# Eight value buffers in a dilated-attention branch, weight splits moved behind a copy, and a reordered last pair of Strassen products

## The chip, the cores and the metric

The kernel runs on one core of one Trainium2 chip. The time is the device time of one execution in microseconds (us); before the change it is 2152.53 us, the median of 3 runs (2151.78 to 2155.79).

## The reference, cut to what matters

A decoder trunk of two residual layers works on 1024 tokens of width 1024, all in float32. Each layer is a token mixer and then a gated MLP. The first layer's mixer puts a chunked gMLP and a mixture of dilated attentions side by side; the second layer's mixer is a gated linear attention.

```
h = rms_norm(x, norm_mix_g[layer])
mix = even_mixer(...) if layer % 2 == 0 else gla_mixer(...)
x = x + mix
h = rms_norm(x, norm_ffn_g[layer])
x = x + (silu(causal_dwconv(h @ w_gate, conv_w, conv_b)) * (h @ w_up)) @ w_down
```

Two places of it matter here. In `even_mixer` eight heads of width 64 take q, k and v from one projection; q and k are normalised, and every query attends to a near window (128 keys back) and to dilated windows. In the MLP the gate and up projections have 2816 columns each.

## The kernel before, in words

**Numbers.** Every matrix product is made of float32r parts: an operand is split into a rounded part and the rest (`split`, lines 101 and 102: a copy on ScalarE, a subtraction on VectorE; `scaled`, lines 106 and 107, also multiplies by a gain), and three of the four products of parts are summed (`PASSES`), so that one 128-row step costs three matmuls.

**Order of the instructions.** The program is traced in the order of the code, and the framework then sets each engine's own order when the program is built, by a simulated timeline: what is traced first goes first, but what is ready sooner in the simulation may overtake. Two calls fix parts of that order. `tc.keep_in_program_order(ins)` puts an instruction behind the one traced before it on its engine. `tc.issue_after(ins)` puts all instructions of a block that run on the engine of `ins` behind `ins`; it is an order, not a wait for a result, and it binds that engine alone. Tiles come from pools; a tile with `bufs=k` has k slots, and a new tile waits until the last reader of the old one in its slot is done.

**The attention (`attention`, called by `even`).** The eight heads are taken as four pairs. `project(p)` does one pair. For each of eight blocks of 128 tokens, `projected(n)` multiplies with the pair's weights into a PSUM bank `pj` (line 193 through `mm_tok`; two banks of that tag, two more for the first pair), squares q and k on ScalarE (line 780), copies the values scaled into `vN` (line 782; six slots), stores them to DRAM (line 785), and normalises q and k in place on VectorE (line 789, which reads the same `pj` bank). The loop over `n` then makes a near-branch "unit": q and k are split, transposed (lines 809 and 817), scored (line 727), masked (line 732), exponentiated (line 733), transposed again (line 747) and multiplied with the value tiles `vN[n-1]` and `vN[n]` into a bank `po` (line 755). Every fourth unit is followed by a copy of `po` (line 828). The first pair is traced three blocks ahead (`lead`). Then `dilated(p)` does the other branch, with values read back from DRAM, while the projection of the next pair is traced after it.

The weights of pair p come from `load_qkv`: four loads into `raw` buffers (line 111; four slots in all), each split into two tiles. Pairs 0 and 2 put their first four tiles in a pool of their own, `wx` (four slots), all others go to the shared eight-slot pool `w`. So the splits for the third pair can begin as soon as the first pair has finished with its `wx` tiles.

**The MLP's gate and up products (`ffn_up`).** Two blocks of 128 columns of one matrix, against 1024 tokens, are one two-by-two step of Winograd's form of Strassen's method: seven products, numbered 1 to 7 (`step(p)`, line 293), on three banks. Product 2 has bank A; 5 and then 3 add up in bank C; 1, 6, 7 and 4 add up in bank B, and between each two of these ScalarE copies the partial sum out of the bank (lines 297, 301, 305 and 308), which the next product must wait for. Product 3 is read from bank C by VectorE (line 310). The units alternate gate and up (`todo`, 22 of them per layer). In the middle ones product 1 of the next unit is traced between 7 and 4. The first unit (gate, whose followers' first products were made earlier) and the last (up) have nothing there:

```
            if 0 < i < len(todo) - 1:
                nxt = stream(*todo[i + 1])
                nxt[0](1)
            step(4)
            step(3)
```

After a gate unit comes the convolution (`conv`, lines 320 to 323); after an up unit the product of both (line 378), the right sides of the down projection and their stores. `ffn_down` (line 400) follows in new PSUM pools over the same banks.

Of the kernel before, what the change touches and what calls it, by code (L numbers as in the profile page):

```python
# [9 lines left out]
F32 = mybir.dt.float32  # L10
# [9 lines left out]
P = 128  # L20
# [20 lines left out]
PASSES = ((0, 0), (0, 1), (1, 0))  # L41


def f32(ap):
    return ap.bitcast(F32)
# [11 lines left out]
def trunk(ctx: ExitStack, tc: tile.TileContext, a, out):  # L57
    nc = tc.nc
    V, A, G, T, Q = nc.vector, nc.scalar, nc.gpsimd, nc.tensor, nc.sync
# [49 lines left out]
    def load_raw(src, name, cols=D):  # L109
        raw = rawp.tile([P, D], F32, tag="raw", name=name)[:, :cols]  # L110
        Q.dma_start(raw, src)
        return raw
# [128 lines left out]
    def ffn_up(l, T3, ps, pool, norm_end):  # L241
        cw = pool.tile([P, NF, 3], F32, name=f"cw{l}")
        Q.dma_start(cw, a["conv_w"][l])
        cb = pool.tile([P, NF], F32, name=f"cb{l}")
        Q.dma_start(cb, a["conv_b"][l])
        right = {1: hq[0][0], 2: hq[1][0], 3: hq[1][1], 4: hq[0][1], 5: T3[0], 6: T3[1], 7: T3[2]}

        def stream(kind, f):

            raws = [load_raw(w_of(kind)[l, f + i], f"r{kind}{f + i}") for i in range(2 if f else 1)]  # L250
            A11, A12, A21, A22 = (raws[i][:, c] if f or not i else None for i in range(2) for _, c in HALVES)
            out = pool.tile([P, 2, S], F32, tag=kind, bufs=1, name=f"{kind}{f}")
            (C11, C12), (C21, C22) = ([out[:, i, c] for _, c in HALVES] for i in range(2))
            s1 = pool.tile([P, 512], F32, tag="s1", bufs=2, name=f"s1{kind}{f}")
            sums, bank, made = {}, {}, {}

            def summed(name, x, y, op):
                sums[name] = pool.tile([P, 512], F32, tag="S", bufs=4, name=f"{name}{kind}{f}")
                G.tensor_tensor(sums[name], x, y, op=op)  # L259
                return sums[name]  # L260

            def left(p):
                if p == 5:
                    return summed("S1", A21, A22, ALU.add)
                if p == 6:
                    return summed("S2", sums["S1"], A11, ALU.subtract)
                if p == 7:
                    return summed("S3", A11, A21, ALU.subtract)
                if p == 3:
                    return summed("S4", A12, sums["S2"], ALU.subtract)  # L270
                return {1: A11, 2: A12, 4: A22}[p]

            def prep(p):
                if f == 0 and p > 2:
                    w = wp.tile([P, 2, 512], F32R, tag="w", name=f"w{kind}{f}p{p}")
                    Q.dma_start(f32(w), sided[l][kind, p])
                    made[p] = [w[:, i, :] for i in range(2)]
                else:
                    made[p] = parts_of(left(p), f"w{kind}{f}p{p}")

            def step(p):
                if p not in made:
                    prep(p)
                L = made[p]

                b = {2: "A", 5: "C", 3: "C"}.get(p, "B")
                more = b in bank
                if not more:
                    bank[b] = ps.tile([P, 512], F32, tag="pt" if b == "A" else "m1", name=f"p{kind}{b}{f}")
                o = bank[b]  # L290
                for j in range(4):
                    for ii, jj in PASSES:
                        T.matmul(o, L[ii][:, j * P : j * P + P], right[p][:, jj, j, :], skip_group_check=more,  # L293
                                 start=(not more and j == 0 and (ii, jj) == PASSES[0]),
                                 stop=(j == 3 and (ii, jj) == PASSES[-1]))
                if p == 1:
                    A.copy(s1, o)
                elif p == 2:
                    V.tensor_add(C11, s1, o)
                elif p == 6:  # L300
                    A.copy(C12, o)
                elif p == 5:
                    A.copy(C22, o)
                elif p == 7:
                    A.copy(s1, o)  # L305
                    V.tensor_add(C22, C22, s1)  # L306
                elif p == 4:
                    A.copy(C21, o)  # L308
                elif p == 3:
                    V.tensor_add(C12, C12, o)  # L310

            return step, out, prep

        def conv(f, g2):
            ts = []
            for i in range(2):
                g = g2[:, i, :]
                t = pool.tile([P, S], F32, tag="t", bufs=4, name=f"t{f + i}")
                w = lambda j: cw[:, f + i, j : j + 1]
                A.activation(t, g, AF.Identity, bias=cb[:, f + i : f + i + 1], scale=w(2))  # L320
                V.scalar_tensor_tensor(t[:, 1:], g[:, : S - 1], w(1), t[:, 1:], op0=ALU.mult, op1=ALU.add)  # L321
                V.scalar_tensor_tensor(t[:, 2:], g[:, : S - 2], w(0), t[:, 2:], op0=ALU.mult, op1=ALU.add)  # L322
                A.activation(t, t, AF.Silu)  # L323
                ts.append(t)
            return ts

        def put(dst, f, p, src):
            Q.dma_start(dst[l][p][f // 4][:, f // 2 % 2, :], src)

        def down_weights(f):  # L330

            ra, rb = (load_raw(a["w_down"][l, f + i], f"rd{f + i}") for i in range(2))
            A11, A21, A12, A22 = ra[:, :512], ra[:, 512:], rb[:, :512], rb[:, 512:]
            S = {p: pool.tile([P, 512], F32, tag="S", bufs=4, name=f"D{p}{f}") for p in (5, 6, 7, 3)}
            V.tensor_add(S[5], A21, A22)
            V.tensor_sub(S[6], S[5], A11)
            V.tensor_sub(S[7], A11, A21)
            V.tensor_sub(S[3], A12, S[6])
            for p in S:
                put(wsd, f, p, S[p])  # L340

        def down_acts(f, t0, t1):

            (B11, B12), (B21, B22) = ([t[:, c] for _, c in HALVES] for t in (t0, t1))
            x, y = (pool.tile([P, 2, 512], F32, tag="t", bufs=4, name=f"{n}{f}") for n in "xy")
            right = {1: B11, 2: B21, 3: B22, 5: x[:, 0], 6: x[:, 1], 7: y[:, 0], 4: y[:, 1]}
            V.tensor_sub(right[5], B12, B11)
            V.tensor_sub(right[6], B22, right[5])
            V.tensor_sub(right[7], B22, B12)
            V.tensor_sub(right[4], B21, right[6])  # L350
            for p in right:
                put(actd, f, p, right[p])

        todo = [(kind, f) for f in range(0, NF, 2) for kind in "gu"]
        cur, nxt = stream(*todo[0]), stream(*todo[1])
        for step, _, _ in (cur, nxt):
            step(1)
            step(2)
            if step is cur[0]:
                for prep, p in ((nxt[2], 1), (nxt[2], 2), (cur[2], 5)):  # L360
                    prep(p)
                norm_end()
        for i, (kind, f) in enumerate(todo):
            step, out, _ = cur
            early = (1, 2) if i < 2 else (1,)
            for p in (5, 6, 2, 7):
                if p not in early:
                    step(p)
            if 0 < i < len(todo) - 1:
                nxt = stream(*todo[i + 1])  # L370
                nxt[0](1)
            step(4)
            step(3)
            if kind == "g":
                ts = conv(f, out)
            else:
                for j in range(2):
                    V.tensor_mul(ts[j], ts[j], out[:, j, :])
                down_acts(f, *ts)
                down_weights(f)  # L380
            cur = nxt
# [333 lines left out]
    def attention(ps, at, av, pq, pq0, par0, wx, wq0, gqk, masks, rest, gm_open):  # L715
# [46 lines left out]
        def project(p, ws=None, then=None, early=None):  # L762


            ws = ws or load_qkv(p, wx)
            pool = pq if p % 2 else pq0
            qR = pool.tile([P, 2, S], F32R, tag="qR", bufs=1, name=f"qR{p}")
# [2 lines left out]
            vN, os, qns = [], [], []  # L770
            heads = lambda t: t.rearrange("p (h c) -> p h c", c=64)

            def projected(n):
# [4 lines left out]
                qn = pq.tile([P, 256], F32, tag="qn", bufs=5, name=f"qn{p}{n}")  # L778
                rn = r0[:, n : n + 1]
                A.activation(qn, pj[:, :256], AF.Square, scale=rn)  # L780
                vN.append(pq.tile([P, P], F32, tag="vN", bufs=6, name=f"vN{p}{n}"))
                got = A.mul(vN[n], pj[:, 256:384], rn)
                if early:
                    early(n, got)
# [12 lines left out]
            for n in range(NT):  # L797
# [22 lines left out]
                if n % 4 == 0:  # L820
                    ot, po = outputs(f"{p}n{n}")
# [3 lines left out]
                     lambda s, i: kT[:, 2 * s + i, :].rearrange("p (r m) -> p r m", r=4)[:, :, 32 * m0 : 32 * n + 32],  # L825
                     vN[m0 : n + 1], mband, lambda t: t.rearrange("p (m r) -> p r m", r=4))
                if n % 4 == 3:
                    A.copy(ot[:, :, :P], po)
                if then and n in (4, 5):
                    then(n - 4)  # L830
            v4 = av.tile([P, 4, 2, P], F32, tag="v4", name=f"v4{p}", bufs=1)
# [33 lines left out]
        def combined(p, g, os, den, e):  # L865
# [11 lines left out]
            V.tensor_add(o0, o0, o1)  # L877
            Q.dma_start(bcat[g].rearrange("(n p) c -> p n c", p=P)[:, :, p * P : p * P + P], o0)

        made = project(0, wq0, early=rest)  # L880
        for p in range(PAIRS):
            os, *qkv = made
# [482 lines left out]
```

## Time and profile before

| | before |
|---|---|
| median of 3 runs | 2152.53 us |
| the profiled execution | 2153.15 us |
| its span from first to last instruction | 2151.4 us |
| mean granted TensorE clock over the span | 0.999 |
| TensorE matmul busy | 2126.6 us (99%) |
| VectorE busy | 1526.0 us (71%) |
| ScalarE busy | 1035.9 us (48%) |
| GpSimd busy | 482.4 us (22%) |

The profile is of one execution. PE is TensorE (PEld its weight loads), DVE VectorE, ACT ScalarE, POOL GpSimd, SP the engine that issues the DMAs. A group or timeline row gives the start and the duration in us, the engine, the line, the operation, the tile written and the tiles read, and in brackets how long the engine had been idle before it and what ended that. Matmuls overlap in the array, and their ends are modelled. A row of the view by windows gives the length of a stretch, the busy time of each engine in it with the number of instructions, and then the granted TensorE clock as a share of full speed, the share of DMA time and the GB/s.

### The profile page before, as it was taken

The numbers are of one execution on the slowest core, as the hardware profiler recorded it, in microseconds if no ns is written. First come the engines' busy times: TensorE is split into PE (matmuls) and PEld (weight loads), VectorE is DVE, ScalarE is ACT, GpSimd is POOL, SyncE is SP. The second block draws the span as 40 slices with busy tenths as digits, with TensorE's granted clock in tenths as the row PEclk, the third lists the DMA queues.
The fourth block names the chain that finished last, engine by engine and source line by source line (L and its number), as shares of the span: only waits on it lengthen the run. The fifth ranks groups of instructions, "written<-read, shape, count | busy, mean of one in ns | idle before, by whom it ended". The sixth has DMA issues, their size and how long they took to land.

```text
span 2151.4 us, 29696 instructions
## 1 busy us (share of the span) xinstructions
PE 2126.6 (99%) x10444; PEld 1804.0 (84%) x10444; DVE 1526.0 (71%) x2451; ACT 1035.9 (48%) x1998; POOL 482.4 (22%) x521
## 2 busy tenths in 40 slices
PE   8999999999999999999999999999999999999999
PEld 7999988888888888888898888888788888888887
DVE  7566655587888888655577777677778888885554
ACT  7555664365444444444454455535544444444443
POOL 5344310012424334000010011011234334220000
PEclk9999999999999999999999999999999999999999
DMA  7022313754444544765553233395554544457664
GB/s 273 24 77 68 104 40 120 256 195 156 155 161 158 176 143 157 255 237 192 206 183 113 74 105 102 133 307 206 177 167 161 168 153 154 162 181 280 215 216 166
DMA packets 159413, 353.70 MB, mean 164 GB/s; under 512 B 17392, under 2 KB 54256, under 8 KB 158880
## 3 DMA queue, kind: packets, MB, share of 16 engines
q1 hardware_dynamic: 159264, 351.81, 47.9%
q8 instruction: 82, 1.34, 0.3%
q14 instruction: 67, 0.55, 0.1%
HBM read 243.15 MB, written 108.59 MB: 163 GB/s over the span
## 4 chain that ended last, share of the span: by engine, by line
PE 92%; DVE 2%; ACT 2%; DMA 2%; issue 1%; SPq 0%; POOL 0%; DVEq 0%; ACTq 0%
PE puB L293 11%; PE pgB L293 11%; PE po L193 8%; PE pv L193 6%; PE pj L193 6%; PE puC L293 6%; PE pgC L293 6%; PE pdB L400 5%; PE pdC L400 5%; PE pdO L400 4%; PE puA L293 3%; PE pgA L293 3%; PE pdQ L400 2%; PE pdP L400 2%; PE pu L193 2%; PE pBq L1070 2%
## 5 line engine op out<-in xcount | busy, mean ns | idle before, releaser
L102 DVE TENSOR_TENSOR da<-ar,da 128x512 fp32r<-128x512 f32 x154 | 106.1, 689 | 154.2 <-ACT da L101 154.1
L101 ACT CAST da<-ar 128x512 fp32r<-128x512 f32 x154 | 95.9, 623 | 207.8 <-PE pdC L400 91.5
L193 PE MATMUL po<-wo,hq 128*128 128x512 f32 x768 | 184.0, 394 | 0.2 <-ACT hq L101 0.2
L193 PEld LDWEIGHTS po<-wo,hq 128*128 128x128 f32 x768 | 141.6, 188 | 29.6 <-DVE hq L102 1.1
L193 PE MATMUL pv<-wv,hq 128*128 128x512 f32 (+2 forms) x768 | 140.8, 340 | 1.6 <-DVE b L1102 1.6
L400 PE MATMUL pdB<-dw,da 128*128 128x512 f32 x528 | 135.5, 391 | 0.9 <-ACT u L308 0.7
L400 PE MATMUL pdC<-dw,da 128*128 128x512 f32 x528 | 135.1, 390 | 0.0
L193 PEld LDWEIGHTS pv<-wv,hq 128*128 128x128 f32 x768 | 118.7, 189 | 16.4 <-DVE b L1102 2.1
L400 PEld LDWEIGHTS pdB<-dw,da 128*128 128x128 f32 x528 | 98.7, 188 | 22.3 <-ACT u L308 1.1
L259 POOL TENSOR_TENSOR S1g<-rg 128x512 f32<-128x512 f32 x20 | 31.1, 1555 | 382.9 <-DMA wsd<-D 266.1
L400 PEld LDWEIGHTS pdC<-dw,da 128*128 128x128 f32 x528 | 99.0, 188 | 20.5
L102 DVE TENSOR_TENSOR dw<-wr,dw 128x512 fp32r<-128x512 f32 x154 | 105.6, 686 | 12.1 <-ACT dw L101 11.9
L193 PE MATMUL pj<-wq,hq 128*128 128x384 f32 x576 | 111.3, 341 | 0.0
L141 POOL TENSOR_SCALAR rn<-ssq 128x1 f32<-128x1 f32 x24 | 9.7, 403 | 446.1 <-ACT h L149 244.9
L101 ACT CAST dw<-wr 128x512 fp32r<-128x512 f32 x154 | 95.0, 617 | 15.7 <-DMA wr<-in_w_dn 9.3
L400 PE MATMUL pdO<-dw,da 128*128 128x512 f32 x396 | 102.2, 389 | 0.2 <-DVE dw L102 0.2
L193 PEld LDWEIGHTS pj<-wq,hq 128*128 128x128 f32 x576 | 99.9, 189 | 0.1
L400 PEld LDWEIGHTS pdO<-dw,da 128*128 128x128 f32 x396 | 74.2, 188 | 16.0 <-DVE dw L102 0.6
L322 DVE SCALAR_TENSOR_TENSOR t<-g,cw,t 128x1022 f32<-128x1022 f32 x44 | 76.6, 1742 | 0.1
L306 DVE TENSOR_TENSOR g<-g,s1g 128x512 f32<-128x512 f32 x22 | 16.2, 737 | 76.9 <-ACT s1g L305 76.9
L321 DVE SCALAR_TENSOR_TENSOR t<-g,cw,t 128x1023 f32<-128x1023 f32 x44 | 58.2, 1322 | 16.2 <-ACT t L320 16.1
L323 ACT ACTIVATE t<-t 128x1024 f32<-128x1024 f32 x44 | 46.7, 1061 | 29.7 <-DVE t L322 29.6
(1084 smaller groups left out, 5432.6 us busy)
## 6 DMA issues: line engine op xcount, KB each, us to landing
ar<-actd SPq DMA_DIRECT2D x70, 512.0 KB, 3.5
rd<-in_w_down SPq DMA_DIRECT2D x44, 512.0 KB, 3.6
wsd<-D SPq DMA_DIRECT2D x88, 256.0 KB, 2.3
rg<-in_w_gate SPq DMA_DIRECT2D x42, 512.0 KB, 3.6
ru<-in_w_up SPq DMA_DIRECT2D x42, 512.0 KB, 4.5
wr<-wsd SPq DMA_DIRECT2D x40, 512.0 KB, 4.3
actd<-t SPq DMA_DIRECT2D x66, 256.0 KB, 2.2
wr<-in_w_dn SPq DMA_DIRECT2D x30, 512.0 KB, 4.8
```

What stands on the lines that cost most here:

```text
L101: (hi or A.copy)(dst[0], src)
L102: (lo or V.tensor_sub)(dst[1], src, f32(dst[0]))
L141: G.tensor_scalar(r, ssq, 1.0 / n, EPS, op0=ALU.mult, op1=ALU.add)
L193: T.matmul(o, L[i], R[jj][:, sl], start=(k == 0 and (ii, jj) == PASSES[0]), stop=(k == nk - 1 and (ii, jj) == PASSES[-1]))
L259: G.tensor_tensor(sums[name], x, y, op=op)
L293: T.matmul(o, L[ii][:, j * P : j * P + P], right[p][:, jj, j, :], skip_group_check=more, start=(not more and j == 0 and (ii, jj) == PASSES ...
L306: V.tensor_add(C22, C22, s1)
L321: V.scalar_tensor_tensor(t[:, 1:], g[:, : S - 1], w(1), t[:, 1:], op0=ALU.mult, op1=ALU.add)
L322: V.scalar_tensor_tensor(t[:, 2:], g[:, : S - 2], w(0), t[:, 2:], op0=ALU.mult, op1=ALU.add)
L323: A.activation(t, t, AF.Silu)
L400: T.matmul(o, L[ii][:, t * P : t * P + P], R[jj], skip_group_check=more, start=start and not more and (ii, jj) == PASSES[0], stop=stop and ...
L1070: T.matmul(o, L[ii][:, j * P : j * P + P], right[p][:, jj, j, :], skip_group_check=more, start=(not more and j == 0 and (ii, jj) == PASSES ...
```

## The change

Three edits. The value tiles `vN` get eight slots. The weights of the third pair are loaded inside `issue_after` of the copy of line 828 that follows the first pair's fourth unit (`copied[0]`). In the first and the last unit of `ffn_up`, product 3 is traced before product 4 and its first matmul is pinned behind the last matmul of product 7.

```diff
-            def step(p):
+            def step(p, pin=False):
...
-                        T.matmul(o, L[ii][:, j * P : j * P + P], right[p][:, jj, j, :], skip_group_check=more,
-                                 start=(not more and j == 0 and (ii, jj) == PASSES[0]),
-                                 stop=(j == 3 and (ii, jj) == PASSES[-1]))
+                        mm = T.matmul(o, L[ii][:, j * P : j * P + P], right[p][:, jj, j, :], skip_group_check=more,
+                                      start=(not more and j == 0 and (ii, jj) == PASSES[0]),
+                                      stop=(j == 3 and (ii, jj) == PASSES[-1]))
+                        if pin and j == 0 and (ii, jj) == PASSES[0]:
+                            tc.keep_in_program_order(mm)
...
-            step(4)
-            step(3)
+                step(4)
+                step(3)
+            else:
+                step(3, pin=True)
+                step(4)
...
+            if p == 2:
+                with tc.issue_after(copied[0].ins):
+                    ws = load_qkv(p, wx)
             ws = ws or load_qkv(p, wx)
...
-                vN.append(pq.tile([P, P], F32, tag="vN", bufs=6, name=f"vN{p}{n}"))
+                vN.append(pq.tile([P, P], F32, tag="vN", bufs=8, name=f"vN{p}{n}"))
...
-                    A.copy(ot[:, :, :P], po)
+                    copied.append(A.copy(ot[:, :, :P], po))
...
+        copied = []
         made = project(0, wq0, early=rest)
```

## Prediction

> **What bounds the kernel now.** I read the page first: the busy times and the chain that ended last.
>
> ```profile
> PE 2126.6 (99%) x10444; PEld 1804.0 (84%) x10444; DVE 1526.0 (71%) x2451; ACT 1035.9 (48%) x1998; POOL 482.4 (22%) x521
> PE 92%; DVE 2%; ACT 2%; DMA 2%; issue 1%; SPq 0%; POOL 0%; DVEq 0%; ACTq 0%
> ```
>
> TensorE is busy for 2126.6 of 2151.4 us and carries 92% of the chain. The change takes no matmul away, so it can win only where TensorE stands still (24.8 us in all, start and end included) or runs below its full clock. The view of TensorE's waits names those places; the columns after the colon are the total, the number of times and the longest.
>
> ```profile
> PE pj L193 <- ACT wx L106: 5.8, 1, 5.8
> PE puB L293 <- ACT s1u L305: 1.4, 2, 0.7
> PE po2d L755 <- DVE pT2d L752: 0.8, 1, 0.8
> PE pP0n L747 <- ACT sm0n L733: 0.8, 1, 0.8
> PE pdB L400 <- ACT u L308: 0.7, 1, 0.7
> ```
>
> The 5.8 us are the first weights of the first pair, at the start; no edit touches them. The second row is the last up unit of each layer, and the fourth lies in the first pair's attention. The view by windows of 1 us shows what surrounds it; the number after POOL's count is the granted clock.
>
> ```profile
> 48.00:49.00 1.00, 0.69 (x7) 0.47 (x6) 1.00 (x4) 0.62 (x2) 0.48 (x2) 1.00 0.72 151
> 49.00:50.00 1.00, 0.40 (x4) 0.25 (x4) 1.00 (x5) 1.00 (x4) 1.00 (x2) 1.00 0.90 320
> 50.00:51.00 1.00, 0.77 (x4) 0.53 (x5) 1.00 (x3) 1.00 (x5) 0.76 (x3) 1.00 0.83 332
> 51.00:52.00 1.00, 0.77 (x8) 0.54 (x6) 0.89 (x4) 0.55 (x4) 1.00 (x2) 1.00 0.29 92
> 52.00:53.00 1.00, 0.91 (x8) 0.91 (x8) 0.76 (x3) 1.00 (x4) 1.00 (x3) 0.87 0.87 307
> 53.00:54.00 1.00, 1.00 (x6) 1.00 (x6) 0.52 (x2) 0.55 (x3) 0.15 (x1) 0.50 0.14 47
> 54.00:55.00 1.00, 1.00 (x7) 1.00 (x7) 0.48 (x1) 0.23 (x1) 0.17 (x1) 0.50 0.00 0
> 55.00:56.00 1.00, 1.00 (x8) 1.00 (x8) 0.85 (x3) 0.21 (x1) 0.30 (x1) 0.50 0.23 66
> 56.00:57.00 1.00, 1.00 (x7) 1.00 (x7) 1.00 (x4) 1.00 (x5) 0.78 (x2) 0.92 0.00 0
> ```
>
> For five microseconds TensorE (first number after the length) is only partly busy while VectorE and ScalarE are nearly full: it loses 0.31 + 0.60 + 0.23 + 0.23 + 0.09 = **1.46 us**. Then its clock falls to one half: 0.13 + 3 x 0.50 + 0.08 = **1.71 us** more. Together 3.17 us. Over the whole span the mean clock is 0.999 (the table ahead of this), about 2.2 us lost, so nearly all of the clock's loss lies here.
>
> **Eight value slots.** The timelines of ScalarE, VectorE and TensorE (in this order) say why TensorE had no work there.
>
> ```profile
> 43.86 1.14 ACT L106 ACTIVATE wx<-wq20r,g 128x384 fp32r<-128x384 f32 x2 [0.53 <-PE pj L193]
> 48.67 0.47 ACT L780 ACTIVATE qn<-pj,r 128x256 f32<-128x256 f32 x1
> 53.87 0.37 ACT L782 ACTIVATE vN<-pj,r 128x128 f32<-128x128 f32 x1 [0.45 <-PE po0n L755]
> 60.94 0.37 ACT L782 ACTIVATE vN<-pj,r 128x128 f32<-128x128 f32 x1
> 66.06 0.58 ACT L828 COPY ot0n<-po0n 128x512 f32<-128x512 f32 x1
> 68.60 0.47 ACT L780 ACTIVATE qn<-pj,r 128x256 f32<-128x256 f32 x1 [1.97 <-PE pj L193]
> 71.58 0.37 ACT L782 ACTIVATE vN<-pj,r 128x128 f32<-128x128 f32 x1 [2.51 <-PE po0n L755]
> ```
> ```profile
> 45.92 1.14 DVE L107 SCALAR_TENSOR_TENSOR wx<-wq21r,g,wx 128x384 fp32r<-128x384 f32 x2
> 50.15 0.61 DVE L107 SCALAR_TENSOR_TENSOR wq<-wq13r,g,wq 128x384 fp32r<-128x384 f32 x1
> 54.27 0.48 DVE L789 SCALAR_TENSOR_TENSOR qn<-pj,r,rq 128x256 f32<-128x256 f32 x1 [0.75 <-ACT vN L782]
> 61.34 0.48 DVE L789 SCALAR_TENSOR_TENSOR qn<-pj,r,rq 128x256 f32<-128x256 f32 x1 [3.75 <-ACT vN L782]
> ```
> ```profile
> 48.18 0.41 PE L193 MATMUL pj<-wq,hq 128*128 128x384 f32 x1
> 55.85 3.87 PE L193 MATMUL pj<-wq,hq 128*128 128x384 f32 x20
> 123.58 2.38 PE L193 MATMUL pj<-wx,hq 128*128 128x384 f32 x12
> ```
>
> The first pair's last projection ends at 48.18 + 0.41 = 48.59, and the next, the second pair's first, begins at 55.85. Its weights are whole at 50.15 + 0.61 = 50.76. What it lacks is a bank. The two `pj` banks hold blocks 7 and 8, and VectorE's pass over a block (line 789) comes only after the value copy (line 782). With six slots the seventh copy takes the slot of the first value tile, which unit 2 still reads: it waits for `po0n` and runs at 53.87. The eighth runs at 60.94, after unit 3, though its block had been squared at 48.67. With eight slots neither has to wait: the seventh value copy can stand beside its square, the eighth at about 49.1, right behind the 48.67 row.
>
> So the second pair's projection may start near 48.6 and fill the gap. It takes its weight tiles one after the other: at 3.87 us for 20 matmuls a block of 24 takes about 4.6 us, and the tile finished at 50.76 is wanted only after 21 of them, at 52.7. Two blocks, some 9 us, may be early. With TensorE full from 48 to 53 nothing should bring the clock down. I count **both losses as gone: -3.17 us**. Bounds: 0, if the scheduler keeps its order, and 3.17 + 0.8, if the `po2d` wait in the third pair goes too. The same slots free banks at each change of pair, so I take half of that wait as an estimate, **-0.40 us**. What is late next is the units' own chain on ScalarE and VectorE: blocks run early leave less matmul work later to cover it (see the rivals).
>
> The longest single wait here is 0.8 us, and the clock fell all the same; that is the row against part of this sum. The Trainium skill, "TensorE: Matmul & The Clock Gate", section "HAM oscillation — how this bites in real kernels", has the clock drop only after gaps above about 3.4 us. The rows here disagree with it; by that rule the clock's loss would not be the gap's, and the sum would keep 1.71 us of it.
>
> **The third pair's splits.** Four splits on ScalarE (two rows like the 43.86 one: 2.3 us) and four on VectorE (2 x 1.14 = 2.3 us) leave 43.9 to 47.1, just where these two engines are full and the gap begins. They go behind the copy at 66.06. ScalarE has 1.97 us of idle time before 68.60 and 2.51 before 71.58, so 2.3 us fit, and the first user is the projection at 123.58, over 50 us later. What the edit saves lies in the same 1.46 us, so it adds nothing of its own: 0. If that cover were gone, four splits in the way of a projection would cost up to 2.3 us; a gain of the same 2.3 us is excluded, as the waits there are already counted. On SP's queue two raw buffers are held some 22 us longer, so two loads of later weights come later; those weights are split after 100, so nobody waits.
>
> **Up's last unit.** TensorE's timeline at the end of layer 1's up products, and below it the first row of layer 2's down products:
>
> ```profile
> 882.86 2.88 PE L293 MATMUL puC<-hq,wu20p 128*128 128x512 f32 x12
> 885.58 2.88 PE L293 MATMUL puB<-T,wu20p 128*128 128x512 f32 x12
> 889.13 3.03 PE L293 MATMUL puB<-hq,wu20p 128*128 128x512 f32 x12 [0.68 <-ACT s1u L305]
> 892.00 1.52 PE L400 MATMUL pdB<-dw,da 128*128 128x512 f32 x6
> ```
> ```profile
> 1937.99 1.66 PE L400 MATMUL pdB<-dw,da 128*128 128x512 f32 x6 [0.68 <-ACT u L308]
> ```
>
> The code says 7, 4, 3, but the scheduler had put product 3 (bank C) before 7, and then 4 waits 0.68 us for 7's partial sum to be copied out of bank B. In the order 7, 3, 4 product 3 runs for 2.7 us between them and hides the copy, in both layers: 2 x 0.68 = **-1.36 us**. Product 7 may come earlier, since a whole product on bank A precedes it. Product 4 stays last, so layer 2's down products still wait 0.68 us for its copy; layer 1's start without waiting (892.00). The PSUM slots may fall differently: one such wait more or less, so -0.68 to -2.04.
>
> **Gate's first unit.** The same edit moves product 3 behind 7 there, where neither waits. TensorE, then ScalarE, then VectorE, in layer 1:
>
> ```profile
> 491.40 2.88 PE L293 MATMUL pgC<-hq,wg0p 128*128 128x512 f32 x12
> 494.12 2.43 PE L293 MATMUL puB<-T,wu0p 128*128 128x512 f32 x10
> 496.39 2.88 PE L293 MATMUL pgB<-T,wg0p 128*128 128x512 f32 x12
> ```
> ```profile
> 502.10 1.06 ACT L323 ACTIVATE t<-t 128x1024 f32<-128x1024 f32 x1
> ```
> ```profile
> 514.10 1.22 DVE L378 TENSOR_TENSOR t<-t,u 128x1024 f32<-128x1024 f32 x1
> ```
>
> Up's product 6 (494.12) can fill the place before 7, so TensorE loses nothing. Product 3, and with it the convolution, comes about 496.39 - 491.40 = 5.0 us later; its silu then ends at 508.2 instead of 503.2, and its user is at 514.10. I cost it at **0**; if nothing fills the place before 7, it costs a copy's wait, 0.68 us in each layer, +1.36.
>
> **The sum.** -3.17 - 0.40 - 1.36 = -4.93 us. The profiled execution took 2153.15 us (span 2151.4 and 1.75 around it), 0.62 above the median of the runs. On that execution 2148.2; on the median **2147.6 us**.
>
> **Rivals.** *The clock stays.* TensorE's gap closes, but the half clock comes at some such place all the same: the 1.71 us remain and the time is 2149.3. For it: a clock that fell without any wait above 0.8 us; against it: it fell right behind the five partly busy rows, and the mean of 0.999 leaves no room for a second drop. The same section of the Trainium skill, and its Part 1, where the activity window runs freely of the program, would make this rival the likelier one.
>
> *The slots do nothing.* The scheduler's simulation may think other work more urgent and leave the projections at 55.85; only up's end gains: 2152.53 - 1.36 = 2151.2. Against it: the seventh copy's wait is a real one, and it goes.
>
> *The hole moves (slower).* Two blocks of projection run early, so their 9 us are missing when the first pair's later units and the dilated units have only ScalarE's and VectorE's chain to feed TensorE, between about 75 and 123 us and again at the next changes of pair. A stretch as at 48 to 57 costs 3.17 us. From 4.93 / 3.17 = 1.6 new stretches on the change is a loss: two give 2147.6 + 6.3 = 2153.9, three 2157.1. For it: every engine's order in 200 us is drawn anew from a simulation; against it: TensorE's waits after 57 us in the attention come to little (the 0.8 us row is the longest).
>
> **How the numbers follow.** A measurement of this kernel tells about 0.2% (4.3 us, below 2148.2 or above 2156.8) from no change. The forecast has 0.62 (its own range 2146 to 2149.5; some 0.50 of it below 2148.2, 0.12 above), the clock 0.08 (0.03 of it below), the slots doing nothing 0.08, the moved hole 0.22 (0.06 with two stretches, 0.16 with three or more). Faster 0.50 + 0.03 = 0.53; same 0.12 + 0.05 + 0.08 + 0.06 = 0.31; slower 0.16. The range leaves out the forecast's best tail (0.04) and the three moved stretches (0.16): 2145.8 to 2155.
>
> **What would show it.** Right: no row below 0.9 for TensorE or its clock between 46 and 60 us; the value copies 7 and 8 next to their squares; a second-pair projection before 52 us; the third pair's splits after the copy; no wait of `puB` for `s1u`; the same total of matmul time. Wrong: a half clock elsewhere before 260 us, a wait of a projection for `wx`, a new wait of `pgB` for ScalarE near 491 us, or a second wait of `pdB` for `u`.

## The result and the profile after

The changed kernel is slower: 2163.51 us, the median of 6 runs (2162.78 to 2169.25), beside 2153.72 for the kernel before in the same runs (2151.78 to 2156.41). The ratio is **1.0050, with a 95% interval of 1.0040 to 1.0061**. The prediction was 2147.6 us, 2145.8 to 2155, so the time lies outside its range and on the other side of no change. The profiled execution of the changed kernel, 2169.25 us (span 2167.5), is its slowest; the other five lie between 2162.8 and 2163.9.

**What was forecast for the start did come.** The view by windows of the changed kernel, where before had its partly busy stretch and its half clock:

```profile
48.00:50.00 2.00, 2.00 (x15) 2.00 (x14) 2.00 (x6) 1.51 (x6) 0.88 (x2) 1.00 0.50 154
50.00:53.00 3.00, 3.00 (x23) 2.95 (x21) 1.62 (x4) 1.20 (x4) 1.69 (x4) 1.00 0.41 98
53.00:56.00 3.00, 3.00 (x19) 3.00 (x18) 0.85 (x2) 1.23 (x3) 1.90 (x4) 1.00 0.51 171
```

TensorE is full and its clock whole. ScalarE's timeline shows why, and where the third pair's splits went:

```profile
42.85 0.47 ACT L788 ACTIVATE qn<-pj,r 128x256 f32<-128x256 f32 x1 [1.34 <-POOL qn L799]
43.22 0.36 ACT L790 ACTIVATE vN<-pj,r 128x128 f32<-128x128 f32 x1
49.25 0.48 ACT L788 ACTIVATE qn<-pj,r 128x256 f32<-128x256 f32 x1
49.62 0.37 ACT L790 ACTIVATE vN<-pj,r 128x128 f32<-128x128 f32 x1
...
71.83 0.58 ACT L836 COPY ot0n<-po0n 128x512 f32<-128x512 f32 x1
72.30 1.13 ACT L106 ACTIVATE wx<-wq20r,g 128x384 fp32r<-128x384 f32 x2
```

The seventh and eighth value copies (line 790) stand right behind their squares (line 788), at 43.22 and 49.62 instead of 53.87 and 60.94, and the splits come after the copy of line 836. Up to 250 us TensorE's idle time and its clock's loss together fall by 3.1 us (10.76 idle and 1.70 of clock before, 9.34 and 0 after).

**The loss lies at 350 to 400 us**, where the attention gives its result to the output projection. First the kernel before, then the changed one, by windows of 10 us:

```profile
350.00:360.00 10.00, 10.00 (x45) 8.31 (x45) 6.11 (x17) 6.37 (x8) 3.02 (x2) 1.00 0.09 28
360.00:370.00 10.00, 10.00 (x49) 8.25 (x48) 7.57 (x13) 6.16 (x11) 0.00 (x0) 1.00 0.85 291
370.00:380.00 10.00, 10.00 (x53) 8.37 (x52) 5.08 (x9) 3.24 (x6) 0.00 (x0) 1.00 0.66 231
```
```profile
350.00:360.00 10.00, 9.15 (x43) 7.36 (x44) 6.25 (x10) 5.44 (x8) 0.00 (x0) 1.00 0.45 126
360.00:370.00 10.00, 6.02 (x26) 4.37 (x25) 9.88 (x30) 6.62 (x11) 1.32 (x1) 0.84 0.62 216
370.00:380.00 10.00, 1.25 (x5) 0.85 (x6) 5.37 (x7) 1.07 (x2) 1.73 (x2) 0.50 0.58 182
380.00:390.00 10.00, 10.00 (x43) 8.32 (x44) 3.00 (x5) 2.15 (x4) 0.00 (x0) 0.81 0.36 130
```

TensorE stands still for 0.85 + 3.98 + 8.75 = 13.58 us, and its clock gives away 1.6 + 5.0 + 1.9 = 8.5 us, so it stood at one half for some 17; 1.9 of the 8.5 (380 to 390) fall under full work. Its waits name the reason:

```profile
PE pc L711 <- DMA cat<-bcat: 8.6, 1, 8.6
PE pj L193 <- ACT wx L106: 5.8, 1, 5.8
PE pc L711 <- DVE mx L685: 2.6, 1, 2.6
```

The second row is the start, as before. The first and third are new: the transposes of the output projection (`pc`) wait for `cat`, the attention's result read back from DRAM, and for `mx`, the gMLP's. Now TensorE's timeline and SP's DMA issues of the changed kernel:

```profile
356.51 5.74 PE L193 MATMUL pu<-wu,hq 128*128 128x512 f32 x24 [0.32 <-ACT ut L696]
366.56 1.29 PE L711 MATMUL pc<-ident,mx 128*128 128x128 f32 x4 [2.57 <-DVE mx L685]
...
377.33 1.11 PE L711 MATMUL pc<-ident,cat 128*128 128x128 f32 x4 [8.63 <-DMA cat<-bcat]
379.87 1.12 PE L450 MATMUL pc<-ident,cat 128*128 128x128 f32 x4 [1.42 <-DMA cat<-bcat]
```
```profile
353.49 0.89 SPq L857 DMA_DIRECT2D od<-ot3d  x2
357.22 0.91 SPq L896 DMA_DIRECT2D on<-od  x2
372.30 0.98 SPq L886 DMA_DIRECT2D bcat<-ot3n  x2
374.66 0.33 SPq L702 DMA_DIRECT2D cat<-bcat  x1
```

and the same issues of the kernel before:

```profile
339.22 0.89 SPq L849 DMA_DIRECT2D od<-ot3d  x2
342.82 0.91 SPq L887 DMA_DIRECT2D on<-od  x2
357.22 3.01 SPq L878 DMA_DIRECT2D bcat<-ot3n  x2
360.64 0.33 SPq L697 DMA_DIRECT2D cat<-bcat  x1
```

This is the attention's **tail**: after the last dilated product its result is stored (`od`), reloaded (`on`), combined with the near branch on VectorE, stored (`bcat`) and loaded again (`cat`), 21 us in both kernels from the first issue to the last. While it runs, TensorE has only the gMLP's u projection (`pu`, 192 matmuls). Before, 107 of these stood behind the last dilated product; they end at 369.70, 9 us after the load of `cat` was issued. After, 24 are left; they end at 362.25, 12 us before that load.

Two rows of TensorE's timelines tell where the others were spent, first before, then after:

```profile
253.62 2.99 PE L193 MATMUL pv<-wv,hq 128*128 128x512 f32 x12
```
```profile
229.95 1.85 PE L193 MATMUL pv<-wv,hq 128*128 128x512 f32 x7
```

The gMLP's v projection starts 24 us earlier, among the third pair's dilated products, and u 16 us earlier, at 294.77 instead of 310.66. The attention's products yield: the last dilated one ends at 352.50 instead of 338.26.

The slots are what lets v in. Its blocks take the same two `pj` banks (`proj512`), so it has to wait until the last pair's blocks have left them. The view of the tile `pj` gives the first and the last start of the value copies, before and after:

```profile
L782 ACT ACTIVATE vN<-pj,r x32: 347/361/383, 19.1 to 253.2; 128x128 f32<-128x128 f32 x32
```
```profile
L790 ACT ACTIVATE vN<-pj,r x32: 346/360/382, 19.1 to 230.9; 128x128 f32<-128x128 f32 x32
```

Before, the last copy stands at 253.2, though its block had been squared at 237.82; after, at 230.9, right behind its square.

A mark for the whole stretch is the eighth store of the first half of the output projection, before and after, in SP's rows:

```profile
422.35 0.39 SPq L433 DMA_DIRECT2D xd<-xh  x1
```
```profile
435.03 0.33 SPq L438 DMA_DIRECT2D xd<-xh  x1
```

12.7 us later. With the 3.1 us gained by 250 us, the tail lost 15.8: 13.58 of idle time, and most of the rest is half clock under work.

### The profile page after: what moved, and what is told of

It is laid out like the page before. It is cut to its first block, busy times and chain, and to the rows that moved or that the text cites. A ratio compares the mean times of both kernels' runs of the same rounds, so it can differ in the third digit from the quotient of the medians.

```text
span 2167.5 us, 29691 instructions
## 1 busy us (share of the span) xinstructions
PE 2128.8 (98%) x10444; PEld 1805.1 (83%) x10444; DVE 1527.6 (70%) x2451; ACT 1038.1 (48%) x2000; POOL 483.7 (22%) x521
## 4 chain that ended last, share of the span: by engine, by line
PE 89%; DMA 3%; DVE 3%; ACT 2%; issue 1%; SPq 0%; POOL 0%; DVEq 0%; ACTq 0%
PE pgB L293 11%; PE puB L293 11%; PE pv L193 6%; PE pj L193 6%; PE pgC L293 6%; PE puC L293 6%; PE pdB L405 5%; PE pdC L405 5%; PE po L193 5%; PE pdO L405 4%; PE puA L293 3%; PE pgA L293 3%; PE pdP L405 2%; PE pdQ L405 2%; PE pu L193 2%; PE pBq L1079 2%
## 5 line engine op out<-in xcount | busy, mean ns | idle before, releaser
L193 PE MATMUL pj<-wq,hq 128*128 128x384 f32 x576 | 117.3, 344 | 0.0
L259 POOL TENSOR_TENSOR S4u<-ru,S2u 128x512 f32<-128x512 f32 x20 | 48.9, 2445 | 54.6 <-DVE wg2p L102 9.6
```

The costliest lines, as they stand in the source:

```text
L193: T.matmul(o, L[i], R[jj][:, sl], start=(k == 0 and (ii, jj) == PASSES[0]), stop=(k == nk - 1 and (ii, jj) == PASSES[-1]))
```

## The experiments

**Theory**: TensorE's independent work (v, then u) is spent early, because the eight slots set the last pair's banks free early; then the tail stands open. **Rivals**: the slots upset the order of the first three pairs; the early v projection costs by itself; another edit is to blame. The intervals below are 95% intervals of the ratio to the kernel before, run beside each.

### One edit at a time

`slots_only` is before with this line alone:

```diff
-                vN.append(pq.tile([P, P], F32, tag="vN", bufs=6, name=f"vN{p}{n}"))
+                vN.append(pq.tile([P, P], F32, tag="vN", bufs=8, name=f"vN{p}{n}"))
```

> Only the eight value slots; splits and up's order as before. Theory (the slots let the gMLP's projections of v and u start early and use up the matmul work that covered the last pair's tail): the whole loss is here, 9 to 13 us over before, with a wait of about 8 us of TensorE for the reloaded attention output between 350 and 400 us, and only some 24 u matmuls left behind the last dilated product. Rival A (the moved splits make the loss): 3 us faster than before. Rival B (the pinned product in gate's first unit makes it): also 3 us faster.

Measured 2165.86 us, ratio 1.0060 (1.0046 to 1.0074). Its waits begin with the same row:

```profile
PE pc L706 <- DMA cat<-bcat: 8.8, 1, 8.8
```

**The slots alone make the whole loss.**

`splits_only` has only the splits' queueing (the `issue_after` block for `p == 2` and `copied`):

> Only the third pair's splits behind the copy, six slots, up's order as before. Theory: within 1.5 us of before; the gap at 48 to 57 us gets smaller by what VectorE's 2.3 us were worth, but the waits of the seventh and eighth value copies stay, and 107 u matmuls are left behind the last dilated product as before. Rival A: 10 us slower. Rival B: no change.

Measured 2156.06 us, ratio 1.0016 (1.0005 to 1.0026): slightly slower, 3.2 us where I had expected at most 1.5. The gap at 48 us is smaller (0.77 us), but the half clock now comes at once and costs 3.4 us instead of 1.7:

```profile
48.00:50.00 2.00, 1.23 (x8) 0.81 (x7) 1.68 (x4) 1.87 (x5) 1.76 (x4) 0.82 0.29 115
50.00:53.00 3.00, 3.00 (x19) 3.00 (x19) 1.16 (x4) 1.84 (x7) 1.48 (x3) 0.50 0.46 131
```

`up_only` has only the order 7, 3, 4 (the edits in `step` and behind `todo`):

> Only the order 7, 3, 4 in the first gate and the last up units. Theory and my sum: 1.1 to 1.4 us faster than before, no wait of product 4 for the copy of product 7's sum. Rival B: 8 us or more slower, with TensorE waiting in gate's first unit near 490 and 1540 us.

Measured 2151.77 us, ratio 0.9997 (0.9989 to 1.0006). The two waits of `puB` for `s1u` are gone from its trace; 1.36 us is inside the interval, but so is nothing.

`no_slots` has both of these and six slots:

> Both other edits, six slots. Theory: the sum of the two alone, 1 to 3 us faster than before. Rivals A and B: slower than before by 8 us or more.

Measured 2153.05 us, ratio 1.0010 (0.9999 to 1.0020): no change, not the 1 to 3 us that I had expected.

### Which pair's slots

In `slots_pair3` only the last pair has eight slots; in `slots_first3`, which is the changed kernel otherwise, the last pair has six:

```diff
-vN.append(pq.tile([P, P], F32, tag="vN", bufs=6, ...))
+vN.append(pq.tile([P, P], F32, tag="vX" if p == 3 and n > 5 else "vN",
+                  bufs=2 if p == 3 and n > 5 else 6, ...))
```
```diff
-vN.append(pq.tile([P, P], F32, tag="vN", bufs=8, ...))
+vN.append(pq.tile([P, P], F32, tag="vX" if p < 3 and n > 5 else "vN",
+                  bufs=2 if p < 3 and n > 5 else 6, ...))
```

> Kernel before with one thing changed: the last pair alone has eight value buffers, the first three keep six. Theory (the fill is spent early): the last pair's banks come free early, the v projection begins among the second-last pair's dilated products, 24 of the 192 u matmuls are left when the last dilated product is in the order (107 before), and the reload of the attention's result stands open: a wait of 8 to 9 us of the transposes for cat, 13 to 14 us idle at 350-400 us, and, as the gap at 48-53 us stays too, 2164 to 2168 us. Rival A (the eight slots of the first three pairs upset the order there): no change, 2152 to 2154 us. Rival B (the early v projection is harmless and the reload is slower for another reason): between them, about 2158 us.

Measured 2169.49 us, ratio 1.0079 (1.0066 to 1.0092): the whole loss, a little above the range expected. The gap at 48 us is still there (1.13 us idle up to 53), though the clock stays whole behind it in this execution. Its longest wait:

```profile
PE pc L706 <- DMA cat<-bcat: 8.7, 1, 8.7
```

> The changed kernel, but the last pair is held to six value buffers; splits and up's order as in the changed kernel. Theory (the fill is spent early): v begins behind the same products as in the kernel before, 95 u matmuls are left behind the last dilated product (107 before, 24 after), which at 0.239 us each is 2.9 us less cover than before and 17 us more than after, so no wait for cat above 1 us; the gain of the first gap (3.1 us) and of up's ends (about 1.1 us) is kept: 2148 to 2150 us. Rival A (the first three pairs' slots make the loss): about 2163 us, with the wait for cat. Rival B (the 2.9 us less cover decides): 2150 to 2153 us with 1 to 3 us idle at 350-400 us.

Measured **2147.46 us, ratio 0.9974 (0.9962 to 0.9985)**. Its longest waits and its window of the tail:

```profile
PE pj L193 <- ACT wx L106: 5.7, 1, 5.7
PE pBq L1079 <- ACT oq L1087: 2.1, 2, 1.1
```
```profile
360.00:370.00 10.00, 10.00 (x54) 8.29 (x53) 6.63 (x12) 5.96 (x11) 0.00 (x0) 1.00 0.84 316
```

No wait for `cat`, TensorE full. The theory's two halves stand in these two runs: the same two slots lose where v is traced next, and win elsewhere. The 2.9 us less of cover, rival B, cost nothing.

`first3_up` is the same without the splits' queueing:

> As slots_first3, but without the queueing of the third pair's splits: eight slots in the first three pairs, six in the last, and up's order 7, 3, 4. If the splits' queueing costs what its run by itself gave (0.05 to 0.26%), this is 1 to 5 us below slots_first3, 2146 to 2149 us. If that loss came only with six slots in the first pair (its half-clock stretch at 50-60 us), the two agree within 1 us.

Measured 2147.58 us, ratio 0.9973 (0.9962 to 0.9984): the same. Both versions beat both kernels; the splits' queueing is worth nothing once the slots are there.

`slots_pair0` and `slots_pairs12` are before with the slots of the first, or of the second and third pair (`p == 0`, `p in (1, 2)` in the first of the two diffs):

> Kernel before with eight value buffers in the first pair alone. By the prediction's terms this is the gap at 48 to 56 us and nothing else: 3.17 us below before, 2149 to 2151 us, no row of TensorE or its clock below 0.9 at 46 to 60 us, and no wait for cat (107 u matmuls left behind the last dilated product, as before). Rival (the gap moves to the next changes of pair): idle of over 1 us more in 60 to 250 us and no gain.

> Kernel before with eight value buffers in the second and third pair alone. By the prediction's terms 0.40 us (half of one wait of 0.8 us for pT) or nothing: 2152 to 2154 us, the gap at 48 to 56 us as in before. Rival (the other changes of pair gain as much as the first): 2149 to 2151 us.

Measured 2151.21 us, ratio 0.9988 (0.9979 to 0.9997), and 2151.05 us, ratio 0.9985 (0.9977 to 0.9994). Each gains some 2.5 to 3 us, and together they give nearly what `slots_first3` gives with up's order in it. The first closes the gap: TensorE and its clock are full from 48 to 56 us. The second was more than I expected, and its windows don't explain it by idle time:

```profile
48.00:50.00 2.00, 1.30 (x11) 0.93 (x9) 2.00 (x7) 1.42 (x4) 1.27 (x3) 1.00 0.82 253
50.00:53.00 3.00, 2.26 (x17) 1.78 (x17) 2.63 (x9) 2.54 (x9) 2.76 (x6) 1.00 0.69 238
53.00:56.00 3.00, 3.00 (x26) 3.00 (x25) 2.72 (x8) 2.23 (x9) 1.70 (x5) 1.00 0.21 71
```

The gap is there, 0.70 + 0.74 = 1.44 us, but no half clock followed it. Why the clock stays up there is open, and it can't be all: of the executions with a mean clock of 1.000 alone, `slots_pairs12` has seven with a median of 2150.66 us, and the kernel before beside it ten with 2153.25.

### The early projection held back

`pv_held` keeps eight slots in all pairs, and queues the gMLP's matmuls behind the last pair's second near unit (`done` records each unit's last product):

```diff
-        mixed = gmlp(ps, gm)
+        with tc.issue_after(done["3n1"].ins):
+            mixed = gmlp(ps, gm)
```

> The changed kernel with all eight slots in all pairs, but the v projection's matmuls and the rest of that part are queued behind the last pair's second near unit. Theory (the fill is spent early): 75 of 192 u matmuls are left behind the last dilated product, 7.7 us less cover than before and 12.2 us more than after, so most of the 13.6 us at 350-400 us goes: 2149 to 2153 us. Rival A (the eight slots themselves make the last pair late, by the order of copies on ScalarE): the wait for cat stays above 5 us and the time above 2160 us. Rival B (holding v only moves the idle time to 230-260 us, where nothing else is ready): idle of 3 us or more there, 2155 to 2160 us.

Measured 2153.88 us, ratio 1.0001 (0.9992 to 1.0010), 0.9 us above the range expected. Ten of the 13.6 us go, by order alone and with the slots in place:

```profile
350.00:375.00 25.00, 21.52 (x95) 17.48 (x94) 19.64 (x44) 11.34 (x19) 2.59 (x2) 0.93 0.58 207
```

3.48 us are left: a wait of 1.0 us for `cat` and one of 2.5 us of the first output product for a split of `hq` on VectorE; a half clock that costs 1.7 us follows. Rival B is out: from 229 to 260 us TensorE is idle for 0.13 us.

### Between the two: seven slots

`seven_all` is before with `bufs=7`:

> Kernel before with seven value buffers in every pair: 46 u matmuls are left behind the last dilated product, between the 24 of the changed kernel and the 75 of the one that held v back. Theory (what is left of u sets the open part of the reload): 22 matmuls of 0.239 us are 5.3 us more cover than the changed kernel's, so 7 to 9 us idle at 350 to 400 us of its 13.6, and 2156 to 2162 us. Rival (early v alone costs the same however much of u is left): 13 us idle and 2163 to 2167 us.

Measured 2164.09 us, ratio 1.0050 (1.0037 to 1.0062). **This expectation missed**: 46 matmuls left instead of 24, and the same loss. The last dilated product did end 6.1 us ahead of the changed kernel's (346.40), but `cat` was loaded only 1.9 us ahead. The rest had gone into the combination, as VectorE's timeline of the changed kernel can show:

```profile
360.12 0.17 DVE L866 TENSOR_TENSOR cM<-ot3n,on 128x8 f32<-128x8 f32 x1 [1.38 <-DMA on<-od]
360.20 1.29 DVE L102 TENSOR_TENSOR wo<-wo00r,wo 128x512 fp32r<-128x512 f32 x2
361.41 0.16 DVE L869 TENSOR_TENSOR cE<-cM,ot3n 128x8 f32<-128x8 f32 x1
...
370.75 2.13 DVE L885 TENSOR_TENSOR ot3n<-ot3n,on 128x512 f32<-128x512 f32 x2
```

Between its small instructions stand the splits of the output weights `wo`, eight of some 0.65 us; before has them after the combination, from 364.78 on. A combination that lies late is crossed by work that in the kernel before came behind it. It isn't longer for that: 12.7 us (360.12 to 372.88) against 12.0 before (347.84 to 359.85), where the gMLP's products stand in it. But a shorter one is possible: in `slots_first3` it takes 8.7 us (344.76 to 353.41).

`after_wo` and `seven_wo` take them out, of the changed kernel and of `seven_all`; `ends` holds the additions that close the combination:

```diff
-        wo = load_half(w[0], "wo0")
+        if l:
+            wo = load_half(w[0], "wo0")
+        else:
+            with tc.issue_after(ends[-1].ins):
+                wo = load_half(w[0], "wo0")
```

> The changed kernel with one thing more: the splits of the output weights wo (eight on VectorE) are queued behind the combination of the two branches, in which they stood before. The open part of the reload is (end of the combination) minus (end of u). Theory (the tail is late products plus a stretched combination): in the changed kernel's trace the combination takes 12.7 us, 360.1 to 372.8, with eight splits of 0.65 us in it, 5.2 us; where none stands in it it took 8.6 us. So the wait for cat falls from 8.6 to 4 to 5 us, and the time by 4 to 5 us, to 2158 to 2160 us. Rival (the open part is the late last product alone; the splits only fill waits of the combination): the wait stays near 8 us and the time near 2163.5 us. A second rival: the wait for cat goes, and the first output product waits as long for wo: the time stays.

Measured 2160.09 us, ratio 1.0031 (1.0019 to 1.0042): 3.4 us below the changed kernel's median, and its eighth store 3.3 us earlier (431.75). The wait for `cat` fell to 3.5 us, even below the 4 to 5 expected, and a part came back as a wait for `mx`:

```profile
PE pc L717 <- DVE mx L691: 5.2, 2, 3.7
PE pc L717 <- DMA cat<-bcat: 3.5, 1, 3.5
```

> The kernel of seven value buffers with the same queueing of wo's splits. In its trace without it the last dilated product ended 6.1 us ahead of the changed kernel's, but its combination took 15 us instead of 12.7 (356.0 to 370.9), so that only 1.9 us of the 6.1 were left. Theory: without the splits the combination takes some 9 us and ends near 365 us, 4 us ahead of the other kernel of this pair, as the count of u matmuls left (46 against 24, 5.3 us) wants it: 2153 to 2157 us. Rival (how much of u is left doesn't matter): the same as the other kernel of this pair.

Measured 2159.85 us, ratio 1.0027 (1.0017 to 1.0038): 4 us better than without, but equal to `after_wo`; the further 4 us didn't come. It loads `cat` only 1.0 us earlier (366.76 against 367.77), as the gMLP's own products on VectorE, 354.3 to 358.0, stand before and in its combination, which takes 10.2 us (356.12 to 366.27) against 8.0 in `after_wo`. So the count of u matmuls left is not the measure by itself. This table, from TensorE's and SP's timelines, has one that is (us; idle is TensorE's at 350 to 400):

| kernel | last dilated product ends | u left | u ends | load of cat issued | cat minus end of u | idle | eighth store |
|---|---|---|---|---|---|---|---|
| before | 338.26 | 107 | 369.70 | 360.64 | -9.1 | 0 | 422.35 |
| slots_first3 | 335.17 | 95 | 363.90 | 355.24 | -8.7 | 0 | 417.22 |
| pv_held | 341.84 | 75 | 365.39 | 361.89 | -3.5 | 3.5 | 424.93 |
| seven_wo | 346.53 | 46 | 362.39 | 366.76 | +4.4 | 8.5 | 430.84 |
| after_wo | 351.51 | 24 | 361.27 | 367.77 | +6.5 | 10.1 | 431.75 |
| seven_all | 346.40 | 46 | 362.29 | 372.73 | +10.4 | 12.7 | 434.01 |
| after | 352.50 | 24 | 362.25 | 374.66 | +12.4 | 13.6 | 435.03 |
| slots_pair3 | 355.06 | 24 | 364.80 | 377.00 | +12.2 | 13.1 | 437.14 |

The idle time rises with the sixth column, the load's issue minus the end of u. The end of u moves by 8 us (361 to 370), the load of `cat` by 22 (355 to 377): by when the tail starts and by how long VectorE takes over it.

## Why the prediction was wrong

**The gap at 48 us: right.** The signs that I had named came: full windows and clock, the copies beside their squares, a projection of the second pair before 52 us, the splits behind the copy, no wait of `puB`. Only the matmul time is not the same (2128.8 us, 2.2 more): more of it ran at half clock. About 3.1 us were gained by 250 us for -3.57. But the half clock, 1.71 of it, was a chance and not a fixed term: 41 of 78 executions of the kernel before show a mean clock below 1.000, and one of eleven of `slots_pair0` (see the last section).

**The splits: 0 was right beside the slots** (`first3_up` equals `slots_first3`), and too kind without them: 0.16% slower.

**Up's end: the mechanism is right.** The waits went in the trace; the size, 1.36 us, is below what `up_only` can tell from nothing. **Gate's first unit:** 0 stands as well as that run can say; the waits of `pgB` for splits of `hq` rose by 0.7 us in the changed kernel's profile, and none is a wait for a copy.

**The sum, -4.93 us, came near for another kernel**: `slots_first3`, whose last pair keeps six slots, gained 5.6 us (0.0026 x 2153.69; 3.2 to 8.2 by its interval). In part that is luck: the second and third pair gave 2.7 us where the sum had 0.40, the first 2.5 where it had 3.17, and up's 1.36 can't be told from nothing.

**The step that failed** is the one on the changes of pair: "The same slots free banks at each change of pair, so I take half of that wait as an estimate, -0.40 us", with 0 and 3.17 + 0.8 as bounds. I had left a loss out of these bounds. For three pairs the work that the free banks let in is the next pair's projection, which the next units need anyway. Behind the last pair it is v and u, the only matmuls that were left for the tail. The sign there is the other one: `slots_pair3`, which has that change alone, loses 15.8 us (2169.49 against 2153.69). At the second and third pair the sign was right and the size too small (2.7 us in `slots_pairs12`).

**The rival "the hole moves" had the right sign, the wrong place and the wrong price.** Blocks run early did leave a later stretch uncovered, but at 350 to 400 us, not at 75 to 123; and it was one hole of 15.8 us, not two or three of 3.17. I had priced it by the only hole that the profile showed. The price stood elsewhere in the trace of before: from the last dilated product to `cat` lie over 20 us of stores, loads and VectorE, hidden by 107 matmuls, with 9 us to spare. TensorE did not wait there, so no view of waits named it, and the sum was built on waits and on the clock alone. That the splits of `wo` would come to stand in the combination (3.4 us by `after_wo`) could not be read from before.

**Behind the tail** the profiled execution of the changed kernel lost 3.4 us more (1734.2 us from its eighth store to its end against 1730.8 before). Its trace shows where: 1.85 us more of idle time, and a second half clock, 1.70 us, behind some partly busy microseconds at the start of layer 2's MLP:

```profile
1540.00:1550.00 10.00, 9.31 (x35) 7.42 (x34) 8.79 (x15) 5.72 (x15) 0.08 (x1) 0.83 0.44 166
```

The other five executions have a mean clock of 0.996 against 0.995 here, which leaves room for the tail's 8.5 us alone.

**What stays open:** why the combination's remaining waits shift as they do between `after_wo` and `seven_wo`, and where the gain of `slots_pairs12` lies.

## What to carry to other kernels

More buffers let work start early, and the work that starts early is the filler on which a later, latency-bound tail lives: before freeing a resource, list what is traced next behind it, and ask what covers the tail once that is spent. For each chain through DRAM, note how much independent work stands behind its last producer and when that ends; the slack is a bound on what may be moved ahead (here 9 us, less the 2.7 us from the load's issue to the first transpose of it in the changed kernel, 374.66 to 377.33). Give the buffers where they gain (three pairs of four here) and keep them from where they only drain the filler.

## What the runs showed of the hardware

**The half clock is not a fixed consequence of a gap.** Of 78 executions of the kernel before that lay beside the experiments, 37 show a mean granted clock of 1.000 (median 2152.43 us) and 41 one of 0.998 or 0.999 (medians 2154.35 and 2154.01): the same instructions, 1.6 to 1.9 us apart. `no_slots` has it stronger: five of its eleven runs at a clock of 1.000 lie between 2151.26 and 2152.48 us, five at 0.997 or 0.998 between 2156.95 and 2158.79. Its profiled execution is one of the latter; its windows of 2 us:

```profile
246.00:248.00 2.00, 1.95 (x18) 1.94 (x18) 0.88 (x3) 1.95 (x6) 1.36 (x2) 1.00 1.03 420
248.00:250.00 2.00, 0.51 (x5) 0.29 (x3) 1.29 (x4) 0.41 (x2) 1.83 (x4) 1.00 1.01 343
250.00:252.00 2.00, 2.00 (x13) 1.64 (x12) 1.67 (x6) 2.00 (x8) 1.31 (x3) 0.68 0.75 221
252.00:254.00 2.00, 2.00 (x12) 2.00 (x12) 0.37 (x2) 0.88 (x4) 0.23 (x1) 0.50 0.06 19
...
260.00:262.00 2.00, 2.00 (x8) 1.56 (x8) 0.00 (x0) 0.00 (x0) 0.00 (x0) 0.77 0.44 115
```

TensorE was idle for 1.5 us, and its clock stood at one half for about 10. In the changed kernel it was some 17, from 366.8 to 383.9: the clock fell behind the wait of 2.57 us, which ends at 366.56, before the one of 8.63 us begins. The Trainium skill, "TensorE: Matmul & The Clock Gate", section "HAM oscillation — how this bites in real kernels", has the clock drop behind gaps of over about 3.4 us. The drop in `after_wo`, which comes 1 us behind a wait of 3.75 us, agrees with that; the drops behind 1.5 and 2.57 us here, and the one of the kernel before, with no wait above 0.8 us, do not.

**Its price comes in steps.** The clock's losses in the profiles are 1.70 us (the kernel before, `up_only`, `pv_held`, and 1540 us in the changed kernel), 3.40 (`splits_only`), 5.10 (`no_slots`), 6.8 (`after_wo`, `seven_wo`) and 8.5 (the tails of the changed kernel, `slots_only`, `slots_pair3` and `seven_all`). So a half clock lasted about 3.4 us or two to five times that; no stretch of another length was seen.
